# A two-layer decoder trunk on one core: the start and the scan re-ordered, and modulation columns summed from transposed weights

## The chip, the core and the metric

The kernel runs on one core of a Trainium2 chip. The metric is the time of one execution on the device in microseconds, the median of three runs. The core's engines are TensorE (PE in the profile; PEld is its loading of weights), VectorE (DVE), ScalarE (ACT), GpSimd (POOL) and SyncE (SP), which only issues transfers here.

## The reference, cut

All is f32: 512 tokens, 1024 channels. Both layers modulate their normed input by a shift and a scale and their output by a gate, all three computed from a conditioning vector c:

```python
mod = jax.nn.silu(c) @ w + b                      # (1024) @ (1024, 3072), per layer
shift, scale, gate = jnp.split(mod, 3, axis=-1)
...
h = rmsnorm(x, norm_g[l]) * (1.0 + scale) + shift
out = gated_deltanet_layer(...) if l == 0 else nsa_layer(...)
x = x + gate * out
```

Layer 0 is a gated DeltaNet: a projection to q, k, v (each with a causal convolution over 4 tokens and silu), to an output gate z and to decays; then a delta rule in chunks with a triangular solve per chunk, a scan over chunks that carries a 128 x 128 state per head, a norm, and an output projection. The stream after it gives shared keys and values; layer 1 is native sparse attention on these, and its own output projection. A last RMSNorm ends it.

## The kernel before, in words

**Dense products.** Channels lie on partitions, tokens in the free dimension. Each weight tile of 1024 x 128 is loaded (512 KB, tile `wraw`, a ring of three) and split into a high and a low part in fp32r (`split_w`), as is the activation. One output tile of 128 channels x 512 tokens is then 8 x 3 matmuls of 512 columns: high weight on high activation, low on high, high on low (`dense_steps`, lines 190, 192, 194). The high part is made on ScalarE; the low one by a subtraction on VectorE and GpSimd, or, with `adds`, by a negated copy on ScalarE and a transfer of GpSimd's queue that adds the weight to it (line 164).

**Order.** The order on TensorE is written by hand. Latency-bound work (the decay tables, the inverse, the doubling, the scan) is written with calls of `fill(n)` in it, each of which issues the next n matmuls from the list `todo` of dense tiles. `Ahead` wraps a tile, loads its weights one or two tiles early and splits them. ScalarE's order is by hand too in the middle of the program; those of VectorE, GpSimd and SyncE come from a scheduler with priorities (`tc.high_priority`).

**Stages of layer 0.** First the gain (1 + scale) x norm of layer 0 is summed on TensorE from four chunks of modulation weights (`chunk`, `vec_mat`, `ada`: matmuls at line 334 in four row groups, a copy on VectorE at 336, transposes at 340, a reduction at 341). Behind each chunk, x times its gain is split (`xsh`, `xsl`) and two of eight row blocks of the first four key tiles are accumulated in four open banks (lines 450 to 452). Key tiles 4 to 7 follow (`key`), with the shift sums. The list `todo` then holds queries 0 to 2, output gates 0 to 3, query 3, values 0 to 3, queries 4 to 7, values 4 to 7, gates 4 to 7. Each query, key and value tile has convolution taps on VectorE (line 81). Between them run the decay tables and a 32 x 32 triangular inverse on VectorE, which is doubled on TensorE, `attn` for two groups of four heads, and `scan_step(n, G)` for four chunk pairs n and two groups G. `scan_norm` normalises the result. The output projection (`residual`, tiles x10 to x17) begins inside the scan: its first three tiles (`w0`, `p0`, `some`, lines 1054 to 1058) take the first halves of the rows as soon as they exist.

**Modulation pieces.** Everything but layer 0's gain and shift comes later, in 32 transfers of 512 KB (`ada_piece`, into the ring `wraw`). A piece is two row blocks of 512 columns, and VectorE adds each, times one silu(c) per partition, to a partial sum `ap` (line 81; the first of four pieces begins it on ScalarE). After four pieces, four TensorE transposes (line 387) and a reduction (389) give 512 columns. A piece is worked on when the next is called. `with_pieces` calls it at step 13 and at the end of a tile, for queries, values and gates 4 to 7 (24 pieces); `gate_b` in layer 1 calls the other eight.

## Time and profile before

| | us |
|---|---|
| runs | 794.82, 794.88, 793.02; median 794.82 |
| the profiled execution: its time | 796.41 |
| the profiled execution: its span | 794.6 |
| busy: TensorE, VectorE, ScalarE, GpSimd | 748.1, 567.9, 433.8, 277.3 |
| mean granted clock of TensorE | 0.981 |

The span runs from the first to the last instruction that the profiler saw. Busy times count overlapping instructions of one engine once. The granted clock is TensorE's share of full speed, 1.00 being 2.4 GHz. A wait is put down to the releaser that came last. "Line" is a line of the kernel before; a line such as 81 or 84 is a helper's, and the tile names tell which step it is.

### The profile page before, as it was taken

Reading aid. Unit: us, or ns where it says so; the run is one execution under the profiler, and the core shown is the slowest. Engines: PE = TensorE matmul, PEld = TensorE weight load, DVE = VectorE, ACT = ScalarE, POOL = GpSimd, SP = SyncE. Lnnn points to the kernel's source line nnn. Section 1 sums busy time; section 2 is a strip of 40 time slices with the busy share of each in tenths; the row PEclk is TensorE's granted clock in tenths of the full one; section 3 lists DMA queues with packets and bytes.
Section 4 is the critical chain, followed back from the end, with each engine's and each line's share of the span. In section 5 each row is a group of like instructions: output and inputs, shape, how many; then the busy total and the mean of one; then the engine's idle time right before and its main releaser. Section 6 shows DMA issues by size and latency. Waiting matters only on the chain.

```text
span 794.6 us, 13620 instructions
## 1 busy us (share of the span) xinstructions
PE 748.1 (94%) x4837; PEld 610.0 (77%) x4837; DVE 567.9 (71%) x1487; ACT 433.8 (55%) x955; POOL 277.3 (35%) x302
## 2 busy tenths in 40 slices
PE   3999999989999989799999999999999999999986
...
GB/s 298 392 217 206 60 147 153 180 91 122 201 177 189 229 218 54 196 110 193 207 124 169 106 81 93 93 67 94 93 67 67 67 80 133 107 54 146 28 40 107
DMA packets 41780, 108.38 MB, mean 136 GB/s; under 512 B 4522, under 2 KB 13034, under 8 KB 41712
## 3 DMA queue, kind: packets, MB, share of 16 engines
...
HBM read 103.26 MB, written 5.55 MB: 137 GB/s over the span
## 4 chain that ended last, share of the span: by engine, by line
PE 75%; DVE 11%; DMA 6%; ACT 3%; issue 2%; POOL 1%; SPq 0%; ACTq 0%; DVEq 0%; POOLq 0%
PE z L192 5%; PE z L190 5%; PE z L194 5%; DMA aw<-in_ada_w 4%; PE o L1300 4%; PE pt L1284 4%; PE pc L192 4%; PE pc L194 4%; PE pc L190 4%; PE x L194 2%; PE x L192 2%; PE x L190 2%; PE q L192 2%; PE q L194 2%; PE q L190 2%
## 5 line engine op out<-in xcount | busy, mean ns | idle before, releaser
L84 POOL TENSOR_TENSOR wlo<-wraw,whi 128x512 fp32r<-128x512 f32 (+2 forms) x60 | 95.2, 1589 | 120.7 <-ACT whi L87 71.3
L87 ACT ACTIVATE arX<-arX,nm 128x256 f32<-128x256 f32 (+3 forms) x128 | 71.2, 556 | 104.3 <-DVE nm L1241 103.7
L87 ACT ACTIVATE whi<-wraw 128x1024 fp32r<-128x1024 f32 (+2 forms) x85 | 88.3, 1040 | 37.5 <-DMA wraw<-in_wS 9.9
L78 POOL TENSOR_SCALAR arX<-arX,f 128x256 f32<-128x256 f32 (+3 forms) x128 | 68.0, 544 | 99.4 <-DVE f L84 53.7
L194 PE MATMUL z<-h1l,whi 128*128 128x512 f32 x192 | 76.8, 400 | 0.0
L190 PE MATMUL z<-h1h,whi 128*128 128x512 f32 x192 | 76.6, 399 | 0.0
L192 PE MATMUL z<-h1h,wlo 128*128 128x512 f32 x192 | 75.9, 396 | 0.0
L84 DVE TENSOR_TENSOR wlo<-wraw,whi 128x512 fp32r<-128x512 f32 (+3 forms) x57 | 58.5, 1029 | 8.2 <-ACT whi L87 8.0
L81 DVE SCALAR_TENSOR_TENSOR ap<-aw,csil,ap 128x512 f32<-128x512 f32 x56 | 43.7, 781 | 26.7 <-DMA aw<-in_ada_w 25.0
L164 POOL DMA_DIRECT2D wlo<-in_wA x22 | 19.2, 872 | 123.9 <-ACT wlo L87 87.9
L190 PE MATMUL pc<-xh,whi 128*128 128x512 f32 x128 | 52.4, 409 | 3.5 <-DVE vT L81 3.5
L192 PE MATMUL pc<-xh,wlo 128*128 128x512 f32 x128 | 53.1, 415 | 0.0
L194 PE MATMUL pc<-xl,whi 128*128 128x512 f32 x128 | 52.1, 407 | 0.0
L1284 PE MATMUL pt<-ident,arX 128*128 128x128 f32 x320 | 45.3, 272 | 0.0
L1284 PEld LDWEIGHTS pt<-ident,arX 128*128 128x128 f32 x320 | 38.8, 140 | 8.3
L192 PEld LDWEIGHTS z<-h1h,wlo 128*128 128x128 f32 x192 | 36.1, 188 | 6.1
L190 PEld LDWEIGHTS z<-h1h,whi 128*128 128x128 f32 x192 | 36.2, 188 | 5.6
L194 PEld LDWEIGHTS z<-h1l,whi 128*128 128x128 f32 x192 | 36.1, 188 | 5.5
L1241 DVE CUSTOM_DVE_ANT_0 arX<-sw,arY 128x256 f32<-128x256 f32 (+2 forms) x48 | 26.7, 556 | 11.6 <-POOL arX L78 6.2
L1270 DVE TENSOR_SCALAR f<-sm 128x3 f32<-128x3 f32 x64 | 15.8, 246 | 24.5 <-ACT arX L87 24.2
L1300 PE MATMUL o<-pta,vb 128*64 128x128 f32 x336 | 32.1, 275 | 0.0
L190 PEld LDWEIGHTS pc<-xh,whi 128*128 128x128 f32 x128 | 24.7, 193 | 8.7 <-issue 3.9
...
## 6 DMA issues: line engine op xcount, KB each, us to landing
wraw<-in_wB SPq DMA_DIRECT2D x33, 512.0 KB, 3.3
aw<-in_ada_w SPq DMA_DIRECT2D x32, 512.0 KB, 4.9
wraw<-in_wA SPq DMA_DIRECT2D x28, 512.0 KB, 3.6
wlo<-in_wA POOLq DMA_DIRECT2D x22, 512.0 KB, 7.1
wraw<-in_wO SPq DMA_DIRECT2D x8, 512.0 KB, 4.0
...
wraw<-in_wP SPq DMA_DIRECT2D x8, 512.0 KB, 3.3
wraw<-in_wKV SPq DMA_DIRECT2D x6, 512.0 KB, 3.3
```

The costliest lines, as they stand in the source:

```text
L78: eng.tensor_scalar(out=o, in0=i, scalar1=s1, scalar2=s2, op0=op0, op1=op1)
L81: nc.vector.scalar_tensor_tensor(out=o, in0=i, scalar=s, in1=j, op0=op0, op1=op1)
L84: eng.tensor_tensor(out=o, in0=a, in1=b, op=op)
L87: nc.scalar.activation(o, i, fn, **kw)
L164: nc.gpsimd.dma_start(lo, src, accum_op=ALU.add)
L190: nc.tensor.matmul(ps, wh[:, k], xh[:, k], start=(k == 0), stop=False)
L192: nc.tensor.matmul(ps, wl[:, k], xh[:, k], start=False, stop=False)
L194: nc.tensor.matmul(ps, wh[:, k], xl[:, k], start=False, stop=(k == KT - 1))
L1241: nc.vector.tensor_tensor_reduce(out=o, in0=ps, in1=bias, op0=ALU.add, op1=ALU.min, scale=1.0, scalar=init, accum_out=acc)
L1270: nc.vector.tensor_scalar_max(f[:, qb], sm[:, qb], 1e-30)
L1284: nc.tensor.transpose(self.ps[:, i], x[:, kb * P:(kb + 1) * P], ident)
L1300: nc.tensor.matmul(po[64 * e:64 * e + 64, qb * P:(qb + 1) * P], vv, pts[2 * pr + e, br, kb, qb], start=(kb == 0), stop=(kb == qb), tile_po ...
```

## The change

- **Start.** The gain comes in eight slices of 128 columns, each with its rows of x and of the key weights, one ahead of the product that uses it: `gain_sums`, `gain` and `key_weights` for row block k + 1 are issued around the matmuls of block k. Sums are copied out of PSUM on ScalarE. The key weights that the shift's projection needs later stay where they are, so their second loading (`again`) is gone. The shift sums stand inside key tiles 4 and 5. Some small tables move from GpSimd's queue to SyncE's; the vector of ones is one column.
- **Pieces.** The host stores the modulation weights transposed too (`ada_r`): a piece holds whole rows of 1024 for 128 columns, and one `tensor_tensor_reduce` on VectorE, against silu(c) spread to all partitions (`csr`), gives 128 finished columns. Partial sums, transposes and reductions are gone. There are still 32 pieces of 512 KB: eight with queries 4 to 7, one with each of values and gates 4 to 7, eight with the output projection's tiles 3 to 7 (two, two, two, one, one), and eight in `gate_b`.
- **Order.** Output gate 3 stands behind value 0 instead of before query 3. The values' transposes of head 1 move behind `attn(0)`.
- **Scan.** The scan's own VectorE operations get a high priority (`first`). The multiplications of `scan_norm` for the first group are on ScalarE. The first three output weights are loaded and split early, as three entries `outs`, with the adding transfer.

```diff
+    csr = cp.tile([P, KT * P], F32, name="csr")
+    nc.gpsimd.dma_start(csd.rearrange("k p -> p k"), csil)
+    nc.gpsimd.dma_start(csr, csd.rearrange("k p -> (k p)").partition_broadcast(P))
...
+    def ada_piece():
...
+        q, j = i // 4, i % 4
...
+        w = wp.tile([P, KT * P], F32, name=f"aw{i}", tag="wraw", bufs=3)
+        nc.sync.dma_start(w, A["ada_r"][l, 4 * q + j])
...
         def add():
...
-            if k == 0:
-                part[0] = tp.tile([P, T], F32, name=f"ap{i}", tag="ap", bufs=1) if space is None else space[:, 2048:][:, :T]
-            for e in range(2):
-                c = csil[:, k + e:k + e + 1]
-                if k + e == 0:
-                    act(part[0], w[:, e], scale=c)
-                else:
-                    stt(part[0], w[:, e], c, part[0], ALU.mult, ALU.add)
-            if k == 6:
-                due.append(partial(finish, part[0]))
-
-        def finish(part):
-            ps = bank(f"as{i}")
-            for j in range(4):
-                nc.tensor.transpose(ps[:, j], part[:, j * P:(j + 1) * P], ident)
-            m = mod[:, l, 4 * q:4 * q + 4]
-            nc.vector.tensor_reduce(out=m, in_=ps, axis=AX.X, op=ALU.add)
-            tt(nc.vector, m, m, adab[:, l, 4 * q:4 * q + 4], ALU.add)
-
-        while loaded:
-            loaded.pop(0)()
+            c = 4 * q + j
+            nc.vector.tensor_tensor_reduce(out=w, in0=w, in1=csr, op0=ALU.mult, op1=ALU.add, scale=1.0,
+                                           scalar=adab[:, l, c:c + 1], accum_out=mod[:, l, c:c + 1])
...
+    chunks = [spaces[k // 4][:, k % 4 * 1024:][:, :1024].rearrange("p (k f) -> p k f", k=KT) for k in range(KT)]
+    for k in range(KT):
+        nc.sync.dma_start(chunks[k], A["ada_s"][k])
+        if k == 0:
+            nc.sync.dma_start(ident, A["ident"])
+        nc.sync.dma_start(xT[:, k], xsrc[:, k])
+        nc.sync.dma_start(wk[0][:, k], A["wS"][k])
...
+    def gain_sums(k):
+
         with tc.high_priority(offset=200):
-            ada(0, 8 + 2 * i, chunks[i])
-            stt(gs[:, 0, kk], mod[:, 0, 8 + 2 * i:10 + 2 * i], 1.0, normg[:, 0, kk], ALU.add, ALU.mult)
-        for k in (2 * i, 2 * i + 1):
+            ps = pm.tile([P, P], F32, name=f"gain{k}", tag="m")
+            for i in range(KT):
+                g = i % 4
+                nc.tensor.matmul(ps[32 * g:32 * g + 32], square_of(csil[:, i:i + 1], 32), chunks[k][:, i], start=(i < 4), stop=(i >= 4), tile_position=(0, 32 * g))
+            sums0[k] = tmp(f"gainp{k}", (P, P))
+            act(sums0[k], ps)
+
+    def gain(k):
+
+        with tc.high_priority(offset=200):
+            ps = pm.tile([P, P], F32, name=f"gainc{k}", tag="m")
+            nc.tensor.transpose(ps, sums0[k], ident)
             g = gs[:, 0, k:k + 1]
+            nc.vector.tensor_reduce(out=g, in_=V(ps, 0, [[32, 4]]), axis=AX.X, op=ALU.add)
+            nc.vector.tensor_scalar(out=g, in0=g, scalar1=adab1[:, k:k + 1], scalar2=normg[:, 0, k:k + 1], op0=ALU.add, op1=ALU.mult)
             act(xh[:, k], xT[:, k], scale=g)
             stt(xl[:, k], xT[:, k], g, xh[:, k].bitcast(F32), ALU.mult, ALU.subtract)
-        for k in ((), (0, 1, 2, 3), (4, 5, 6, 7), ())[i]:
-            square(k)
-        if i == 2:
+
+    parts0 = {}
+
+    def key_weights(k):
+        if k % 2 == 0:
+            parts0[k] = [wp.tile([P, 2, T], F32R, name=n, bufs=3) for n in ("whi", "wlo")]
+        hi, lo = (t[:, k % 2] for t in parts0[k - k % 2])
+        act(hi, wk[0][:, k])
+        tt(nc.gpsimd if k % 2 else nc.vector, lo, wk[0][:, k], hi.bitcast(F32), ALU.subtract)
+        return hi, lo
+
+    gain_sums(0)
+    gain(0)
+    for k in range(KT):
+        hi, lo = key_weights(k)
+        if k + 1 < KT:
+            gain_sums(k + 1)
+        for i, (w, x) in enumerate(((hi, xh), (lo, xh), (hi, xl))):
+            for c, ps in enumerate(open_ps):
+                nc.tensor.matmul(ps, w[:, c * P:(c + 1) * P], x[:, k], start=(i == 0 and k == 0), stop=(i == 2 and k == KT - 1))
+            if i == 0 and k + 1 < KT:
+                gain(k + 1)
+        for j in ((), (), (0,), (1, 2), (3, 4), (5, 6, 7), (), ())[k]:
+            square(j)
+        if k == 5:
             ps0 = pm.tile([P, T], F32, name="rs0ps", tag="m")
-            nc.tensor.matmul(ps0, ones, acc, start=True, stop=True)
+            nc.tensor.matmul(ps0, square_of(ones), acc, start=True, stop=True)
             rs0 = rows_rstd(ps0, "rs0")
-        wh, wl = split_w(raws[i], 2, split=(i == 0))
-        for c, ps in enumerate(open_ps):
-            for e in range(2):
-                k = 2 * i + e
-                nc.tensor.matmul(ps, wh[:, 2 * c + e], xh[:, k], start=(k == 0), stop=False)
-                nc.tensor.matmul(ps, wl[:, 2 * c + e], xh[:, k], start=False, stop=False)
-                nc.tensor.matmul(ps, wh[:, 2 * c + e], xl[:, k], start=False, stop=(k == KT - 1))
-
-
-    raws = [load_w(A["wA"][4])]
-    shw = []
-    for i, tag in enumerate("XV"):
-        shw.append(chunk(A["ada_w"][0, i], T, arenas[tag]))
-        raws.append(load_w(A["wA"][5 + i]))
-    raws.append(load_w(A["wA"][7]))
+
+    shw = [arena(t, f"sh{t}").rearrange("p (k f) -> p k f", k=KT) for t in ("xh", "xl")]
+    raws = []
+    for h in range(4):
+        raws.append(wk[1][:, :, h * P:(h + 1) * P])
+        nc.sync.dma_start(raws[h], A["wA"][4 + h])
+        for k in range(0, KT, 2) if h < 2 else ():
+            nc.sync.dma_start(shw[h][:, k:k + 2], A["ada_w"][0, h][:, k:k + 2])
+    nc.sync.dma_start(rows, A["rows"].partition_broadcast(P))
+    for t, n in ((cst, "cst"), (wab, "wab"), (rbt, "rb"), (pos, "pos")):
+        nc.sync.dma_start(t, A[n])
+
...
+    def key(h, *between):
+
+        between = list(between)
+        if h < 4:
+            ps = open_ps[h]
+        else:
+            for i, ps in enumerate(dense_steps(None, xsh, xsl, f"pc{h}", 2, raw=raws[h - 4], ahead=False)):
+                if i % 12 == 11 and between:
+                    between.pop(0)()
         kn[h] = tmp(f"kn{h}")
         tt(nc.vector, kn[h], ps, rs0, ALU.mult)
 
...
+    key(4, partial(shift_sums, 0), partial(shift, 0))
+    taps(0, kT[:, 0], kn[0])
+    taps(1, kT[:, 1], kn[1])
+    key(5, partial(shift_sums, 1), partial(shift, 1))
+    xh, xl = by8(arena("xh", "xh", F32R)), by8(arena("xl", "xl", F32R))
+    shifted(0)
+    taps(2, kT[:, 2], kn[2])
+    taps(3, kT[:, 3], kn[3])
+    shifted(1)
+    key(6)
...
-    def with_pieces(steps):
+    def with_pieces(steps, n=1):
 
         for i, s in enumerate(steps):
             if i == 13:
                 ada_piece()
             yield s
-        ada_piece()
+        if n > 1:
+            ada_piece()
 
...
-    for f, heads in ((query, (0, 1, 2)), (gate_proj, (0, 1, 2, 3)), (query, (3,)), (value, (0, 1, 2, 3)), (query, (4, 5, 6, 7)), (value, (4, 5, 6, 7)),
+    for f, heads in ((query, (0, 1, 2)), (gate_proj, (0, 1, 2)), (query, (3,)), (value, (0,)), (gate_proj, (3,)), (value, (1, 2, 3)), (query, (4, 5, 6, 7)), (value, (4, 5, 6, 7)),
                      (gate_proj, (4, 5, 6, 7))):
         todo += [Ahead(f(h), early=f is not query or h > 1) for h in heads]
+    w0 = {}
+
+    def ahead_x1(j):
+
+        raw = load_w(A["wO"][j])
+        yield None
+        w0[j] = split_w(raw, src=A["wO"][j])
+        yield None
+        p0.append((pd if j < 2 else pm).tile([P, T], F32, name=f"x1{j}", tag="d" if j < 2 else "s"))
+        yield from some(j, range(4), every, False)
+
+    outs = [Ahead(ahead_x1(j), early=True) for j in range(3)]
     fill(7)
 
+    nA = cp.tile([P, 8], F32, name="nA")
+    act(nA, rows[:, 0:8], AF.Exp)
...
-    fill(100)
-    for h in range(2):
-        fill((50, 24)[h])
-        value_rows(h)
+    fill(126)
+    value_rows(0)
+    fill(48)
...
+    first = partial(tc.high_priority, offset=600)
...
-            tt(nc.vector, kd, psk, bc(erest[:, sl4, n], P), ALU.mult)
+            with first():
+                tt(nc.vector, kd, psk, bc(erest[:, sl4, n], P), ALU.mult)
...
-            tt(nc.vector, vN[:, sl4, n], vN[:, sl4, n], bc(rs[:, :, n - n0], P), ALU.mult)
+            if G:
+                tt(nc.vector, vN[:, sl4, n], vN[:, sl4, n], bc(rs[:, :, n - n0], P), ALU.mult)
+            else:
+                for i in range(4):
+                    act(vN[:, i, n], vN[:, i, n], scale=rs[:, i, n - n0:n - n0 + 1])
...
-        for h in (2, 3):
+        for h in (1, 2, 3):
...
-        w0 = [split_w(load_w(A["wO"][j])) for j in range(3)]
-        p0 = [(pd if j < 2 else pm).tile([P, T], F32, name=f"x1{j}", tag="d" if j < 2 else "s") for j in range(3)]
+        p0 = []
...
-        todo += [some(j, range(4), every, False) for j in range(2)]
+        todo += outs[:2]
...
-            todo.append(some(2, range(4), every, False))
+            todo.append(outs[2])
...
-        tiles = [Ahead(t) for t in tiles]
+        tiles = [Ahead(with_pieces(t, 2 if i < 3 else 1)) for i, t in enumerate(tiles)]
```

The first place is the start of TensorE's program; `ada_8` and `gain` are sums of layer 0's gain, `pc` the open banks of the key tiles. Before:

```order
L334 MATMUL ada_8_137<-arX,scb 32x256 x8
L340 MATMUL ada_8c<-ident,ada_8p 128x128 x2
L450 MATMUL pc_132<-xsh,whi 128x512
L451 MATMUL pc_132<-xsh,wlo 128x512
L450 MATMUL pc_133<-xsh,whi 128x512
L450 MATMUL pc_134<-xsh,whi 128x512
L450 MATMUL pc_135<-xsh,whi 128x512
L451 MATMUL pc_135<-xsh,wlo 128x512
L451 MATMUL pc_133<-xsh,wlo 128x512
L451 MATMUL pc_134<-xsh,wlo 128x512
L334 MATMUL ada_10_189<-arX,scb 32x256 x4
L452 MATMUL pc_132<-xsl,whi 128x512
```

Now:

```order
L389 MATMUL gain_141<-asxh,csil 32x128 x8
L397 MATMUL gainc_152<-ident,gainp_150 128x128
L389 MATMUL gain_162<-asxh,csil 32x128 x8
L422 MATMUL pc_132<-xsh,whi 128x512
L422 MATMUL pc_133<-xsh,whi 128x512
L422 MATMUL pc_134<-xsh,whi 128x512
L422 MATMUL pc_135<-xsh,whi 128x512
L397 MATMUL gainc_177<-ident,gainp_171 128x128
L422 MATMUL pc_132<-xsh,wlo 128x512
L422 MATMUL pc_133<-xsh,wlo 128x512
L422 MATMUL pc_134<-xsh,wlo 128x512
L422 MATMUL pc_135<-xsh,wlo 128x512
```

The first key product moved behind the second slice's sums, and a slice now runs through the four banks before the next slice's begins.

The second place is VectorE at `attn(1)`: `qk` products are multiplied into `arN` there, and `pha` is a small norm table. Before:

```order
L81 SCALAR_TENSOR_TENSOR ap_2522<-aw_2495,csil,ap_2522 128x512
L81 SCALAR_TENSOR_TENSOR ap_2522<-aw_2520,csil,ap_2522 128x512
L544 COPY pha<-sstq 128x16 x2
L81 SCALAR_TENSOR_TENSOR ap_2522<-aw_2520,csil,ap_2522 128x512
L84 TENSOR_TENSOR arN_803<-qk_2573,arN_803 128x512
L78 TENSOR_SCALAR nx_2557<-pha 128x32
L81 SCALAR_TENSOR_TENSOR ap_2522<-aw_2601,csil,ap_2522 128x512
L84 TENSOR_TENSOR arN_803<-qk_2579,arN_803 128x512
L303 TENSOR_SCALAR pha<-nx_2557 128x32
L84 TENSOR_TENSOR arN_803<-qk_2585,arN_803 128x512
L81 SCALAR_TENSOR_TENSOR ap_2522<-aw_2601,csil,ap_2522 128x512
L84 TENSOR_TENSOR arN_803<-qk_2591,arN_803 128x512
```

Now (an ISA row is a piece, with `mod 128x1` as its sum's read-out):

```order
L542 COPY pha<-sstq 128x16 x2
L78 TENSOR_SCALAR nx_2545<-pha 128x32
L303 TENSOR_SCALAR pha<-nx_2545 128x32
L78 TENSOR_SCALAR pha<-pha 128x32
L84 TENSOR_TENSOR arN_854<-qk_2561,arN_854 128x512
L81 SCALAR_TENSOR_TENSOR nw_2546<-pha 128x32
L340 ISA aw_2711,mod<-aw_2711,csr,colp 128x1024
L340 ISA mod 128x1
L84 TENSOR_TENSOR arN_854<-qk_2567,arN_854 128x512
L84 TENSOR_TENSOR nw_2546<-nw_2546,nx_2545 128x32
L84 TENSOR_TENSOR arN_854<-qk_2573,arN_854 128x512
L84 TENSOR_TENSOR arN_854<-qk_2579,arN_854 128x512
```

Five additions for pieces became one row sum between the same products.

The third place is SyncE's queue from the last layer 0 tiles into the output projection (`aw` a piece, `wraw` a weight). Before:

```order
L370 DMA aw_2495<-in_ada_w 128x1024
L370 DMA aw_2520<-in_ada_w 128x1024
L370 DMA aw_2601<-in_ada_w 128x1024
L370 DMA aw_2648<-in_ada_w 128x1024
L370 DMA aw_2709<-in_ada_w 128x1024
L370 DMA aw_2761<-in_ada_w 128x1024
L370 DMA aw_2791<-in_ada_w 128x1024
L370 DMA aw_2820<-in_ada_w 128x1024
L156 DMA wraw<-in_wO 128x1024 x6
L1076 DMA arK<-in_xT 128x2x512 x2
L156 DMA wraw<-in_wO 128x1024 x2
```

Now:

```order
L336 DMA aw_2494<-in_ada_r 128x1024
L156 DMA wraw<-in_wO 128x1024
L336 DMA aw_2589<-in_ada_r 128x1024
L156 DMA wraw<-in_wO 128x1024
L336 DMA aw_2711<-in_ada_r 128x1024
L156 DMA wraw<-in_wO 128x1024
L336 DMA aw_2787<-in_ada_r 128x1024
L156 DMA wraw<-in_wO 128x1024 x3
L1094 DMA arK<-in_xT 128x2x512 x2
L336 DMA aw_3163<-in_ada_r 128x1024
L336 DMA aw_3185<-in_ada_r 128x1024
L156 DMA wraw<-in_wO 128x1024
```

Three output weights moved in between the pieces, and pieces now follow among the later output weights.

## Rows read from the trace of the kernel before

**Rows 1.** The page: busy time by engine, and the chain that ended last.

```profile
PE 748.1 (94%) x4837; PEld 610.0 (77%) x4837; DVE 567.9 (71%) x1487; ACT 433.8 (55%) x955; POOL 277.3 (35%) x302
...
PE 75%; DVE 11%; DMA 6%; ACT 3%; issue 2%; POOL 1%; SPq 0%; ACTq 0%; DVEq 0%; POOLq 0%
```

**Rows 2.** Windows: PE, PEld, DVE, ACT, POOL busy (instructions), PE clock, DMA share, GB/s.

```profile
20.00:40.00 20.00, 18.47 (x106) 12.91 (x107) 11.86 (x23) 13.75 (x20) 5.42 (x4) 1.00 1.01 392
40.00:60.00 20.00, 18.56 (x99) 12.54 (x98) 18.75 (x23) 6.99 (x10) 15.94 (x12) 1.00 0.69 211
160.00:180.00 20.00, 16.48 (x207) 13.92 (x207) 9.48 (x11) 10.25 (x14) 4.59 (x5) 0.66 0.42 94
280.00:300.00 20.00, 16.25 (x100) 14.23 (x99) 12.87 (x39) 5.35 (x17) 0.86 (x1) 0.91 0.75 200
320.00:340.00 20.00, 14.39 (x85) 12.50 (x84) 16.93 (x35) 7.64 (x21) 8.97 (x8) 0.83 0.63 211
```

**Rows 3.** Waits by engine: us in total, times, longest us.

```profile
PE x L1056 <- DVE wlo L84: 5.5, 1, 5.5
...
PE pc L190 <- DVE vT L81: 3.5, 1, 3.5
...
DVE ap L81 <- DMA aw<-in_ada_w: 25.0, 14, 5.4
...
POOL S L84 <- PE qs L915: 21.9, 2, 16.6
```

**Rows 4.** TensorE's timeline, start: start us, us, line, operands, count, [idle before].

```profile
8.70 1.08 PE L334 MATMUL ada<-arX,scb 128*32 128x256 f32 x8 [8.70 <-DMA arX<-in_ada_s]
...
9.93 1.08 PE L334 MATMUL ada<-arX,scb 128*32 128x256 f32 x8 [0.15 <-DMA arX<-in_ada_s]
...
15.12 0.80 PE L450 MATMUL pc<-xsh,whi 128*128 128x512 f32 x1 [2.87 <-ACT xsh L87]
...
16.14 1.48 PE L450 MATMUL pc<-xsh,whi 128*128 128x512 f32 x3
...
33.50 1.08 PE L450 MATMUL pc<-xsh,whi 128*128 128x512 f32 x4
...
34.41 1.02 PE L444 MATMUL rs0ps<-rs0acc,ones 128*128 128x512 f32 x2
...
41.36 1.92 PE L334 MATMUL ada<-arX,scb 128*32 128x512 f32 x16
...
50.52 0.39 PE L190 MATMUL pc<-xsh,whi 128*128 128x512 f32 x1
```

**Rows 5.** Timelines of VectorE and ScalarE, start.

```profile
12.68 0.16 DVE L81 SCALAR_TENSOR_TENSOR gs<-mod,colp 128x2 f32<-128x2 f32 x1
...
14.37 1.32 ACT L87 ACTIVATE xsh<-arA,gs 128x512 fp32r<-128x512 f32 x2
```

**Rows 6.** Groups by form: busy us, mean ns of one, idle before.

```profile
L84 DVE TENSOR_TENSOR wlo<-wraw,whi 128x512 fp32r<-128x512 f32 x47 | 47.5, 1013 | 2.3 <-ACT whi L87 2.0
...
L81 DVE SCALAR_TENSOR_TENSOR ap<-aw,csil,ap 128x512 f32<-128x512 f32 x56 | 43.7, 781 | 26.7 <-DMA aw<-in_ada_w 25.0 <-ACT ap L87 1.3
...
L81 DVE SCALAR_TENSOR_TENSOR sl<-arK,colp,sh 128x512 fp32r<-128x512 f32 x8 | 11.8, 1481 | 3.8 <-ACT sh L87 3.8
...
L1241 DVE CUSTOM_DVE_ANT_0 arX<-sw,arY 128x512 f32<-128x512 f32 x16 | 11.0, 690 | 8.1 <-POOL arX L78 6.2 <-PE sw L1233 0.9 <-PE sd L1233 0.4
...
L81 DVE SCALAR_TENSOR_TENSOR arK<-x,mod,arK 128x512 f32<-128x512 f32 x8 | 6.0, 747 | 6.1 <-PE x L194 4.5 <-PE x L1058 1.6
...
L387 PE MATMUL as<-ident,ap 128*128 128x128 f32 x32 | 4.8, 274 | 0.0
```

**Rows 7.** VectorE's timeline in the inverse.

```profile
145.04 0.75 DVE L81 SCALAR_TENSOR_TENSOR arA<-pc,colp,arA 128x509 f32<-128x509 f32 x1 [0.72 <-ACT arA L87]
```

**Rows 8.** DMA issues: queue, count, KB each, median us to landing.

```profile
aw<-in_ada_w SPq DMA_DIRECT2D x32, 512.0 KB, 4.9
...
x1d<-arK ACTq DMA_DIRECT2D x8, 256.0 KB, 2.4
```

149 lines of the change are left out of this document (53 added, 96 removed).

## The prediction

> **What bounds the kernel now.** I read four views, each for one question. First the page's busy times: TensorE is busy for 748.1 of 794.6 us [rows 1], so what it issues in the dense products can't shrink much, and a gain has to come from its idle time, from half-rate stretches, or from instructions that it need not issue. The page's chain confirms it: three quarters of the path that ended last is TensorE, 11% VectorE, and 6% DMA, of which the modulation pieces are most [rows 1]. So I looked next where TensorE is not full, by windows of 20 us [rows 2], and then for the cause of each hole in the waits by engine [rows 3]. Four places stand out:
> - The start. The first key product runs at 15.12 us, and the fifth key tile, the first that is an ordinary dense tile, begins at 50.52 us [rows 4].
> - 160 to 180 us: one wait of 3.5 us for a convolution tap on VectorE [rows 3], and a mean granted clock of 0.66 behind it [rows 2], between the two levels of 1.2 and 2.4 GHz, so that some two thirds of the stretch ran at the lower.
> - 280 to 300 us, the second half of the scan: 16.25 of 20 us busy, clock 0.91 [rows 2].
> - 320 to 340 us: 14.39 of 20 us busy, clock 0.83 [rows 2]; the low half of an output weight comes 5.5 us late from VectorE [rows 3].
>
> The profiled execution took 796.41 us, 1.59 above the median of 794.82. The sum is made against 796.41 and the 1.59 is taken off at its end.
>
> **The start.** Before, the gain comes in four chunks of 256 columns, the key weights in four parts. After, everything comes in eight slices of 128 columns, each 1 MB (512 KB of modulation weights, 256 KB of x, 256 KB of key weights). The DMA engines moved 392 GB/s from 20 to 40 us [rows 2], so a slice takes 2.6 us of them and the last lands at about 8.7 + 7 x 2.6 = 27 us, before TensorE can use it. The first row sums can begin when the first chunk did, at 8.70, and take at most the 1.08 of the wider ones [rows 4]: 9.78. From the end of the second half of the sums before (9.93 + 1.08 = 11.01 [rows 4]) to the finished gain (12.68 + 0.16 = 12.84 [rows 5]) lie 1.83 us; a scaled slice of x is another 0.66, half of 1.32 [rows 5]. So the first key product starts at 9.78 + 1.83 + 0.66 = 12.3 us. The first products before ran three in 1.48 us [rows 4]; twelve of these are 5.9, to 18.2. Later four take 0.91 (33.50 to 34.41 [rows 4]), so a slice is 12 x 0.23 = 2.76 us, with half of 1.08 for the next sums and 0.15 for one transpose (4.8 us over 32 [rows 6]): 3.45. Seven of them end at 42.4; the sum of squares adds 1.02 [rows 4], to 43.4. The fifth key tile thus starts 7.1 us earlier than at 50.52. But the first shift sums, 1.92 us before it [rows 4], now stand inside it: **5.2 us** gained. Bounds: 8 with sums half as long and no half-rate products, and 0, because VectorE was busy for 18.75 of 20 us from 40 to 60 [rows 2] and could simply become what the key tiles wait for. I take the sum, since the copies of the sums leave VectorE for ScalarE, which was busy for only 6.99 us there [rows 2].
>
> The re-load of 4 MB of key weights disappears behind other work: nothing. The shared silu row adds a small write and a 512 KB spread read on GpSimd's queue, but the first piece comes with the fifth query tile, twelve dense tiles of 5.5 us after the keys: nothing.
>
> **The doubling stall.** TensorE has the same steps to fill up to the 3.5 us wait [rows 3]. On VectorE the inverse, with convolution taps woven in, is the same chain but for one wait of 0.72 us on ScalarE [rows 7]. I take **0.7**. Bounds: 0, and 3.5 + 16.48 x 0.34 = 9.1 if the whole stall and the slow stretch behind it go [rows 2, 3].
>
> **Scan.** Before, 24 of the 32 pieces fall on the projections beside the scan, two per tile; after, 16, with one per value and gate tile. VectorE waited 25.0 us in 14 places for these transfers [rows 3]. The steps of the scan's chain are also put first on VectorE, and a normalisation of sixteen squares goes to ScalarE, busy for 5.35 of 20 us [rows 2]. From 280 to 300 us TensorE lost 3.75 us idle and 16.25 x 0.09 = 1.5 in clock: **5.2** gained. Bounds 2 and 7: with fewer pieces something else in the chain may come late, and the two stretches beside it also have some idle time.
>
> **The output weights at 320 us.** Three tiles are now loaded and split before, ScalarE making the high halves and an adding DMA of GpSimd's queue the low ones. Lost in this window: 5.6 idle and 14.39 x 0.17 = 2.4 in clock, 8.0 [rows 2]. The next late things are short ones, so I leave 1 us for them: **7.0**. Bounds 0 and 8. What is queued on GpSimd matters: the loads that add stand in one queue with multiplications of the state, which waited 21.9 us in two places for TensorE [rows 3].
>
> **Pieces.** Each was two fused multiply-adds of 0.781 us [rows 6], with four transposes and a reduction per four pieces. Now each is one multiplication with a running sum over 1024 elements. The softmax's instructions with a maximum do 512 elements in 0.690 us [rows 6], so I take 1.38; bounds 0.69 (one of that size) and 1.56 (both old ones). Where they stay beside the dense tiles, VectorE has room: nothing. The 32 transposes leave TensorE; their group is 4.8 us busy [rows 6], of which a third are tails under the next product: **3.2** gained, bounds 0 and 4.8.
>
> Eight of them now fall on five output tiles. A tile is 24 x 0.23 = 5.5 us of TensorE, and has 1.01 + 0.75 + 1.48 = 3.24 us on VectorE (a low half, the residual, a shifted square input [rows 6]). Spare: 5 x 5.5 - 5 x 3.24 = 11.4 us. The waits before were 25.0 us over 32 pieces, 0.78 each [rows 3]. 8 x (0.78 + 1.38) = 17.3, so 5.9 us stick out: **minus 5.9**. Bounds: 0 if VectorE may run behind and catch up, and 8 x (25.0/14 + 1.38) - 11.4 = 13.9 if each waits as long as those that waited.
>
> **Sum.** 5.2 + 0.7 + 5.2 + 7.0 + 3.2 - 5.9 = 15.4; 796.41 - 15.4 = 781.0, and less 1.59 it is **779.4 us**.
>
> **Rivals.**
> - *The doubling stall goes.* The swapped gate and value tiles could let VectorE reach the last tap sooner, so that the clock never falls. For it: it needs only 3.5 us. Against: the same instructions stand before it. 8.4 us more than my 0.7: 771.0.
> - *VectorE binds the start.* For it: 18.75 of 20 us [rows 2]. Against: it loses copies. The 5.2 fall away: 784.6.
> - *The early halves are not early.* The adding loads sit behind a state multiplication on GpSimd's queue and the wait at 320 us stays as it is, so that the change doesn't do there what it says. 7.0 fall away: 786.4. Against: they are issued before the second half of the scan.
> - *Slower: pieces hold VectorE in the output projection.* With two pieces in 24 steps, 12 steps apart (2.8 us), and 4.9 us from issue to landing [rows 8], VectorE may stand at each piece with the residual of the tile, whose bank TensorE wants, queued behind. With 4.9 us of wait in each, 8 x (4.9 + 1.38) - 11.4 = 38.8 stand for my 5.9: 812.3. It decides from a wait w with 8 x (w + 1.38) - 11.4 = 21.3 (the other gains), w = 2.7 us. Against: before, where two pieces also stood in each tile, the longest was 5.4 but the mean 1.8 [rows 3].
> - *Slower: small transfers.* If the three transfers of a slice went one behind the other, each would be at least 4.9 + 2 x 2.4 = 9.7 us [rows 8], the last slice landing at 8.7 + 7 x 9.7 = 76.6, the fifth key tile starting at about 82 instead of 43.4: 39 us more, 818. Against: in the same stretch 512 KB transfers flowed at 392 GB/s [rows 2] though one alone takes 4.9 us [rows 8], so many are in flight. The Trainium skill, "DMA: Bandwidth & Descriptors", in its section on measured rates, advises batching DMAs to 1 MiB or more for three quarters of peak, and so speaks against pieces of 256 KB; by it the time would go towards this rival's 818, by the rate in the row it stays at 779.4, and I follow the row.
>
> **How the numbers follow.** Forecast 0.55, stall gone 0.14, start bound 0.13, halves not early 0.07, pieces hold VectorE 0.07, small transfers 0.04. Range: from 765, which is the stall rival's 771.0 less what the upper bounds of start, scan and transposes add (2.8 + 1.8 + 1.6 = 6.2), to 792, which is the halves' rival's 786.4 with the start's 5.2 gone too. It leaves out the two slow cases (0.11) and the tails of the others. 0.3% (2.4 us) is about what a measurement tells from no change. The two slow cases hold 0.11; a part of them with shorter waits, and the corner where several gains fail together, end within it: same 0.03, slower 0.09, faster 0.88.
>
> **What would show it.** First key product near 12.3 and fifth tile near 43.4 us; no TensorE wait for the low half near 320 us, and the 280 to 300 us stretch near full at clock 1.00; no transposes of partial sums; a piece near 1.4 us. Still a wait of about 3 us before the doubling. In the output projection, small TensorE waits for VectorE, 6 us in all. I am wrong if the waits for pieces there are above 2.7 us each, if the key tiles wait for VectorE, or if the wait at 320 us is still there.

## The result, and the profile after

The changed kernel takes 798.38 us (median of 9 runs, 796.77 to 802.68), the kernel before 793.02 in 9 runs of the same comparison (791.09 to 794.88). The ratio is 1.0073, with a 95% interval of 1.0055 to 1.0090: **slower by 0.7%**, where 779.4 was forecast. Executions of one kernel differ by up to 10 us here, so a difference of 2 us or less is read from the intervals, not from two profiles.

The page of the changed kernel: busy times, and the group of the modulation pieces.

```profile
PE 746.1 (94%) x4869; PEld 607.5 (76%) x4869; DVE 557.0 (70%) x1467; ACT 437.8 (55%) x978; POOL 278.1 (35%) x299
...
L340 DVE CUSTOM_DVE_ANT_0 aw<-aw,csr,colp 128x1024 f32<-128x1024 f32 x32 | 43.3, 1352 | 37.8 <-DMA aw<-in_ada_r 31.2
```

TensorE is busy for 2.0 us less than in [rows 1] in a span of the same 794.6 us: what was taken off it went into waits. A piece is one instruction of 1.35 us in the mean, as predicted (1.38); its transfers still hold VectorE for 31.2 us in all.

The windows of 20 us (columns as in [rows 2]) show where:

```profile
60.00:80.00 20.00, 14.54 (x64) 10.87 (x57) 17.08 (x27) 14.36 (x22) 5.11 (x4) 0.83 0.09 27
160.00:180.00 20.00, 16.44 (x169) 14.00 (x168) 15.52 (x16) 11.88 (x14) 6.35 (x6) 0.80 0.50 113
280.00:300.00 20.00, 19.29 (x112) 15.13 (x110) 9.37 (x29) 8.43 (x20) 1.72 (x2) 1.00 0.60 159
320.00:340.00 20.00, 19.55 (x135) 17.06 (x135) 15.16 (x37) 10.32 (x32) 5.60 (x6) 1.00 0.56 174
360.00:380.00 20.00, 17.37 (x76) 13.80 (x74) 16.96 (x22) 6.09 (x9) 8.56 (x6) 1.00 0.80 276
```

and the first of these windows in the kernel before:

```profile
60.00:80.00 20.00, 20.00 (x97) 14.82 (x96) 19.09 (x27) 15.81 (x24) 6.17 (x4) 1.00 0.66 210
```

From 280 to 300 and from 320 to 340 us TensorE is nearly full at clock 1.00, against 16.25 and 14.39 us and lower clocks before [rows 2]: the scan did gain. From 60 to 80 us, which was full before, it is busy for 14.54 us at 0.83, and from 360 to 380, in the output projection, for 17.37. The stretch at 160 to 180 us is as before but for its clock.

The waits of TensorE, and four rows of its timeline at the start:

```profile
PE gain L389 <- DMA asxh<-in_ada_s: 10.8, 3, 5.5
PE shiftc L485 <- ACT shiftp L87: 5.5, 1, 5.5
PE pc L190 <- DVE vT L81: 3.6, 1, 3.6
...
PE kv L192 <- POOL wlo L84: 1.9, 1, 1.9
...
PE kv L190 <- ACT whi L87: 1.7, 1, 1.7
...
PE x L190 <- DVE arK L81: 0.9, 1, 0.9
```

```profile
5.55 0.87 PE L389 MATMUL gain<-asxh,csil 128*32 128x128 f32 x12 [5.55 <-DMA asxh<-in_ada_s]
...
17.90 0.64 PE L389 MATMUL gain<-asxh,csil 128*32 128x128 f32 x16 [4.17 <-DMA asxh<-in_ada_s]
...
48.34 0.50 PE L190 MATMUL pc<-xsh,whi 128*128 128x512 f32 x1
...
69.67 1.12 PE L485 MATMUL shiftc<-ident,shiftp 128*128 128x128 f32 x4 [5.46 <-ACT shiftp L87]
```

The first sums begin at 5.55 us, earlier than the forecast 8.70, and then the third slice's sums stand at 17.90 for a transfer; the fifth key tile begins at 48.34 us (43.4 forecast, 50.52 before [rows 4]); and the second shift sums are waited for 5.5 us. The wait ahead of the doubling is still there, 3.6 us. The last three waits belong to the output projection (`x`) and the key-value tiles behind it (`kv`).

Four groups of matmuls mark the stages (duration in ns, then first and last start in us): the decay sums `psab`, the queries' sums of squares `ssq`, the last state update `su`, and the key-value tiles `kv`.

```profile
L642 PE MATMUL psab<-arA,pha x16: 592/592/617, 84.4 to 85.8; 128*32 128x512 f32 x16
...
L529 PE MATMUL ssq<-sqarA,pha x16: 592/604/617, 243.7 to 280.9; 128*32 128x512 f32 x16
...
L952 PE MATMUL su<-vp,kd x48: 270/275/377, 239.5 to 328.0; 128*128 128x128 f32 x48
...
L190 PE MATMUL kv<-sh,whi x48: 387/389/628, 379.8 to 423.3; 128*128 128x512 f32 x48
```

The same marks, from the same view, of six kernels (us; "before" in two executions, the second is e10; the kernels e6 to e14 are explained below):

| | before | before, again | after | e6 | e7 | e9 | e14 |
|---|---|---|---|---|---|---|---|
| decay sums begin | 77.0 | 76.1 | 84.4 | 78.0 | 77.6 | 72.6 | 72.5 |
| last `ssq` | 272.2 | 270.4 | 280.9 | 276.0 | 273.4 | 275.2 | 269.1 |
| last `su` | 332.9 | 327.5 | 328.0 | 323.0 | 320.3 | 321.3 | 315.4 |
| first `kv` | 381.6 | 376.3 | 379.8 | 375.0 | 372.8 | 374.3 | 367.2 |
| span | 794.6 | 788.9 | 794.6 | 788.9 | 785.7 | 788.5 | 782.4 |

Read by differences: the change loses 7.4 to 8.3 us before the decay sums and 1.3 to 2.2 from there to the last `ssq`; gains 10 to 14 in the second half of the scan (47.1 us from `ssq` to `su`, against 60.7 and 57.1); loses 3.0 from there to the first `kv` and 4.2 in the key-value tiles (50.5 us from the first `kv` to the first query of layer 1, against 46.3 in both); and gains 2.0 to 2.5 in layer 1.

What fills the hole at the start: windows of 2 us of the changed kernel,

```profile
10.00:12.00 2.00, 2.00 (x7) 1.46 (x7) 0.30 (x2) 0.00 (x1) 0.00 (x0) 1.00 1.31 85
12.00:14.00 2.00, 1.73 (x8) 1.08 (x6) 0.35 (x2) 0.00 (x0) 0.00 (x0) 1.00 0.95 88
14.00:16.00 2.00, 0.00 (x0) 0.00 (x0) 0.00 (x0) 0.00 (x0) 0.00 (x0) 1.00 0.96 103
16.00:18.00 2.00, 0.10 (x4) 0.13 (x8) 0.00 (x0) 1.13 (x2) 0.41 (x1) 1.00 0.85 127
```

and two of them in the kernel before:

```profile
10.00:12.00 2.00, 1.45 (x10) 0.42 (x10) 0.42 (x1) 0.00 (x0) 0.00 (x0) 1.00 1.02 382
...
16.00:18.00 2.00, 2.00 (x6) 1.52 (x6) 1.39 (x3) 0.00 (x0) 0.00 (x0) 1.00 1.04 407
```

GpSimd's timeline in the same stretch,

```profile
3.96 1.11 POOL L322 DMA_DIRECT2D csd<-csil  x1 [3.51 <-DVE csil L84]
17.59 0.60 POOL L323 DMA_DIRECT2D csr<-csd  x1 [12.52 <-DMA csd<-csil]
18.29 1.29 POOL L84 TENSOR_TENSOR wlo<-arX,whi 128x512 fp32r<-128x512 f32 x1
```

and the transfer in the list of DMA issues (queue, count, size, us from issue to landing):

```profile
csd<-csil POOLq DMA_DIRECT2D x1, 4.0 KB, 13.3
```

From 10 to 18 us the DMA engines are busy for 85 to 131% of their time by the records and move 85 to 127 GB/s, where the kernel before moved 382 to 410 in the same windows. The one thing in flight that the kernel before didn't have is a write of 4 KB, the silu of c, in single elements: 13.3 us from issue to landing. GpSimd stood 12.5 us for it, with the low half of the second slice's weights queued behind (18.29); and SyncE's queue, which waited 7.2 us for one slice's key weights to land, issued nothing from 9.60 to 16.86 us.

And VectorE from 50 to 66 us:

```profile
50.86 12.45 DVE L81 SCALAR_TENSOR_TENSOR arK<-kn,colp,arK 128x509 f32<-128x509 f32 x11
63.23 0.68 DVE L84 TENSOR_TENSOR kn<-pc,rs 128x512 f32<-128x512 f32 x1
63.83 0.16 DVE L487 TENSOR_REDUCE mod<-shiftc 128x4 f32<-128x16 f32 x1
...
65.44 0.16 DVE L84 TENSOR_TENSOR mod<-mod,colp 128x4 f32<-128x4 f32 x1
```

Eleven convolution taps (12.45 us) and the fifth tile's normalisation stand ahead of the reduction of the first shift sums, which TensorE had ready at 56.6. ScalarE, whose copy of the second shift sums is queued behind work that needs the first shift, is late in turn, and TensorE with it.

### The profile page after: what moved, and what is told of

It is laid out like the page before. It is cut to its first block, busy times and chain, and to the rows that moved or that the text cites. A ratio compares the mean times of both kernels' runs of the same rounds, so it can differ in the third digit from the quotient of the medians.

```text
span 794.6 us, 13653 instructions
## 1 busy us (share of the span) xinstructions
PE 746.1 (94%) x4869; PEld 607.5 (76%) x4869; DVE 557.0 (70%) x1467; ACT 437.8 (55%) x978; POOL 278.1 (35%) x299
## 3 DMA queue, kind: packets, MB, share of 16 engines
HBM read 101.16 MB, written 5.55 MB: 134 GB/s over the span
## 4 chain that ended last, share of the span: by engine, by line
PE 55%; DVE 5%; DMA 3%; ACT 3%; issue 3%; POOL 1%; ACTq 0%; DVEq 0%; POOLq 0%; SPq 0%
PE z L190 5%; PE z L192 5%; PE z L194 5%; PE o L1318 5%; PE pt L1302 4%; DMA aw<-in_ada_r 3%; PE q L194 2%; PE q L192 2%; PE q L190 2%; PE kv L192 2%; PE kv L194 1%; PE kv L190 1%; PE sw L1250 1%; PE sw L1251 1%; PE oc L1333 1%
## 5 line engine op out<-in xcount | busy, mean ns | idle before, releaser
L84 POOL TENSOR_TENSOR wlo<-wraw,whi 128x512 fp32r<-128x512 f32 (+1 forms) x49 | 80.4, 1643 | 89.2 <-ACT whi L87 60.4
L87 ACT ACTIVATE whi<-wraw 128x1024 fp32r<-128x1024 f32 (+1 forms) x77 | 80.6, 1047 | 16.9 <-DMA wraw<-in_wKV 5.8
L192 PE MATMUL z<-h1h,wlo 128*128 128x512 f32 x192 | 76.1, 396 | 0.0
L340 DVE CUSTOM_DVE_ANT_0 aw<-aw,csr,colp 128x1024 f32<-128x1024 f32 x32 | 43.3, 1352 | 37.8 <-DMA aw<-in_ada_r 31.2
L84 DVE TENSOR_TENSOR wlo<-wraw,whi 128x512 fp32r<-128x512 f32 (+1 forms) x45 | 48.6, 1080 | 1.9 <-ACT whi L87 1.7
L1302 PEld LDWEIGHTS pt<-ident,arX 128*128 128x128 f32 x320 | 38.8, 140 | 8.3
L1288 DVE TENSOR_SCALAR f<-sm 128x3 f32<-128x3 f32 x64 | 14.1, 221 | 24.3 <-ACT arX L87 23.9
```

The lines of the kernel that those rows point to most:

```text
L84: eng.tensor_tensor(out=o, in0=a, in1=b, op=op)
L87: nc.scalar.activation(o, i, fn, **kw)
L192: nc.tensor.matmul(ps, wl[:, k], xh[:, k], start=False, stop=False)
L340: nc.vector.tensor_tensor_reduce(out=w, in0=w, in1=csr, op0=ALU.mult, op1=ALU.add, scale=1.0, scalar=adab[:, l, c:c + 1], accum_out=mod[:, ...
L1288: nc.vector.tensor_scalar_max(f[:, qb], sm[:, qb], 1e-30)
L1302: nc.tensor.transpose(self.ps[:, i], x[:, kb * P:(kb + 1) * P], ident)
```

## The experiments

**1. The start, first round.** e1 moves the two transfers of silu(c) behind the key tiles in the text; e2 sets VectorE's order by hand, six taps and then the reduction; e3 is both; e4 has the start of the kernel before with all the rest.

```diff
# e1
-    nc.gpsimd.dma_start(csd.rearrange("k p -> p k"), csil)
...
     dump("h", xT)
+    nc.gpsimd.dma_start(csd.rearrange("k p -> p k"), csil)
# e2
-    key(4, partial(shift_sums, 0), partial(shift, 0))
+    def between_taps():
+        with order("DVE"):
+            for h in range(2):
+                taps(h, kT[:, h], kn[h])
+            shift(0)
+            for h in (2, 3):
+                taps(h, kT[:, h], kn[h])
+
+    key(4, partial(shift_sums, 0), between_taps)
```

> The changed kernel, with the two transfers that spread silu(c) to all partitions issued behind the key tiles instead of first of all. Theory A: the write of 1024 single elements holds the DMA engines from 10 to 18 us, and with it the third slice and, on GpSimd's queue, the low half of the second slice. Then the stretch of 85 to 130 GB/s is gone, the fifth key tile starts at about 41 us instead of 48.3, and the time falls by 5 to 8 us, to about 791. Rival C: slices of 256 and 512 KB are slow in themselves, or VectorE binds the start: the fifth tile stays near 48 and the time near 798.

> The changed kernel, with the order on VectorE fixed so that the shift sums' reduction stands behind six taps instead of eleven. Theory B: the wait of TensorE for the second shift sums (5.5 us) comes from this queue, since ScalarE's copy of the sums stands behind work that needs the first shift. Then this wait is under 1 us, the clock stays up from 60 to 80 us, and the time falls by 5 to 8 us, to about 792. Rival: the taps that are moved back hold the next thing (the low half of a key weight), the wait reappears there, and the time falls by less than 2 us.

> Both edits. If the two losses are separate, as theories A and B say, the gains add up: 12 to 15 us, about 785. If one hides the other (the start is bound by one chain through VectorE), no more than the larger of the two single gains, about 791.

> The start as it was before (four chunks, re-loading of key weights, shift sums ahead of the fifth key tile), with all the rest of the change, and silu(c) spread behind the key tiles. If the start alone is what went wrong, the rest keeps what the traces show behind the start (7.5 us): about 785.5 against 793.0 of the kernel before. Rival: the rest gains only because the start is late and other engines catch up meanwhile; then about 792.

Measured: e1 799.74 (ratio to before 1.0100, 1.0077 to 1.0123), e2 794.77 (1.0028, 1.0010 to 1.0045), e3 794.46 (1.0027, 1.0008 to 1.0045), e4 794.32 (1.0024, 1.0007 to 1.0040). e2 is 3.6 us faster than the changed kernel, half of what was expected: the wait fell from 5.5 to 2.6 us, not away. e1 tested nothing: GpSimd's queue is in the scheduler's order, and the write was issued at 3.90 us again, as it was in e3 and, at 4.57, in e4. So e1 repeats the changed kernel and e3 repeats e2. e4 has the write with the old start, and its decay sums began at 83.3. So the loss before the decay sums needs no new slices.

**2. The row without memory.** e5 makes the spread row on TensorE, e6 adds e2's order, e7 is e4 with that row, e8 is e6 with the eight pieces of the output projection back at values and gates 4 to 7.

```diff
# e5 to e8, after the key tiles
-    nc.gpsimd.dma_start(csd.rearrange("k p -> p k"), csil)
-    nc.gpsimd.dma_start(csr, csd.rearrange("k p -> (k p)").partition_broadcast(P))
+    for i in range(2):
+        ps = pm.tile([P, T], F32, name=f"row{i}", tag="m")
+        for k in range(4):
+            nc.tensor.matmul(ps[:, k * P:(k + 1) * P], square_of(csil[:, 4 * i + k:4 * i + k + 1]), ident, start=True, stop=True)
+        act(csr[:, i * T:(i + 1) * T], ps)
# e8
-        tiles = [Ahead(with_pieces(t, 2 if i < 3 else 1)) for i, t in enumerate(tiles)]
+        tiles = [Ahead(t) for t in tiles]
```

> The earlier edit that put the two transfers of silu(c) later in the text did not move them: the scheduler of GpSimd's queue issued them at 3.9 us again, and the slow stretch stayed. Here the row is made without memory: eight 128-column products of silu(c) with the identity on TensorE and two copies on ScalarE, after the key tiles; about 2 us of new work. Theory A: the stretch of 85 to 130 GB/s between 10 and 18 us is gone, the fifth key tile starts near 41 us and the first decay sums near 78 instead of 84.4, and the time falls by 5 us from that of the changed kernel, to about 793. Rival C (small slices slow in themselves, or a start bound by VectorE): the stretch stays or the fifth tile does, and the time is 798 to 800.

> The row on TensorE, and the reduction of the shift behind six taps instead of eleven, as in the earlier run that gained 3.6 us by itself. If the two are separate: about 790. If the key tiles are bound by VectorE as soon as transfers are early, the second edit or the first gives nothing more and it is about 793.

> The start as before, with the rest of the change, and the row on TensorE: no write of single elements at all. Theory A says that the write also cost the run with the old start its 6 us (decay sums at 83.3 instead of 77.0). Then the decay sums begin near 78 and the time is about 789. If it stays at 794, the rest of the change gains nothing even from an undisturbed start.

> As the run with the row on TensorE and the shift first, but the eight pieces of the output projection are back with values and gates 4 to 7, two in each tile. Theory: those eight cost the output projection and the key-value tiles behind it 5 to 7 us (the predicted 5.9), and their return costs the scan up to 5.2: within 2 us of that run. Rival: the spreading was a loss, and this is faster by 4 us or more; or the scan loses all of its gain, and it is slower by 4 us or more.

Measured: e5 792.00 (1.0000, 0.9985 to 1.0015), e6 792.08 (0.9992, 0.9976 to 1.0009), e7 790.17 (0.9960, 0.9940 to 0.9979), e8 794.00 (1.0019, 0.9993 to 1.0045). In e5 the slow stretch is gone:

```profile
10.00:12.00 2.00, 2.00 (x6) 1.51 (x6) 0.33 (x2) 0.58 (x2) 1.27 (x1) 1.00 1.04 407
12.00:14.00 2.00, 2.00 (x7) 1.52 (x7) 1.17 (x4) 1.24 (x2) 0.00 (x0) 1.00 1.04 398
14.00:16.00 2.00, 2.00 (x23) 1.31 (x22) 0.58 (x1) 0.80 (x2) 0.00 (x0) 1.00 1.03 399
16.00:18.00 2.00, 2.00 (x11) 1.43 (x8) 0.77 (x3) 0.72 (x1) 1.28 (x1) 1.00 1.05 405
```

So the write and the read that waits for it cost 6.4 us (798.38 against 792.00; 5.8 by the ratios), and 4.2 with the old start (e4 against e7; 5.1 by the ratios). These are net of the new row, whose products stand on TensorE from 76.0 to 77.9 us in e5, just ahead of the decay sums. With the write gone, the new slices do what was forecast: the fifth key tile begins at 42.06 us in e5's timeline, but the shift sums are waited for again:

```profile
42.06 0.50 PE L190 MATMUL pc<-xsh,whi 128*128 128x512 f32 x1
...
61.46 0.90 PE L482 MATMUL shiftc<-ident,shiftp 128*128 128x128 f32 x3 [3.52 <-ACT shiftp L87]
```

8.5 us earlier at the fifth key tile than before (7.6 against e10), and no earlier at the decay sums (77.8): all of it is given back on the way, some 2 us of it to the row itself. e6 gained nothing on e5, as its second forecast had it (792.08 against 792.00); its wait for the second shift sums is still 2.6 us. Its trace shows what may hold it up. VectorE of e6, and below it GpSimd at the same time:

```profile
45.56 9.15 DVE L81 SCALAR_TENSOR_TENSOR arK<-kn,colp,arK 128x509 f32<-128x509 f32 x6
54.63 0.68 DVE L84 TENSOR_TENSOR kn<-pc,rs 128x512 f32<-128x512 f32 x1
55.24 0.16 DVE L484 TENSOR_REDUCE mod<-shiftc 128x4 f32<-128x16 f32 x1
...
57.03 5.06 DVE L81 SCALAR_TENSOR_TENSOR arK<-kn,colp,arK 128x509 f32<-128x509 f32 x6
```

```profile
39.32 12.55 POOL L84 TENSOR_TENSOR arA<-arA,rs 128x512 f32<-128x512 f32 x8 [3.39 <-DMA pha<-in_wab]
```

Six taps take 9.15 us, most of it while GpSimd multiplies x by the reciprocal norm (39.32 to 51.87), six later ones 5.06. If this is the chain, six taps ahead of the reduction are still too many, and so is the fifth tile's normalisation (54.63), which stands between them and the reduction; e9 tests it.

e8 against e6, by the marks: from the last `ssq` to the last `su` 53.6 us (280.9 to 334.5) against 47.0, and from there to the first `kv` 48.7 against 52.0, with the `kv` tiles taking 38.8 against 42.5. In these two profiles eight pieces fewer beside the scan are worth 6.6 us there, and cost 7.0 in the output projection and the tiles behind it. The same profiles also differ by 5.4 us between the decay sums and the last `ssq` (203.4 against 198.0), some of it because e8's profiled execution (795.39) was longer than its median and e6's (790.89) shorter. By the medians the move is worth 1.9 us, within the 2 that were expected, and the intervals overlap.

**3. The shift ahead, and what carried the scan.** e9 is e6 with the reduction behind three taps only and ahead of the normalisation. e10 is the kernel before, once more, for its profile. e11 is e7 with the first three output weights loaded and split late, as before; e12 is e7 without the scan's priority on VectorE and with all of `scan_norm` there.

```diff
# e9
+    dve = ExitStack()
+
+    def between_taps():
+        dve.enter_context(order("DVE"))
+        taps(0, kT[:, 0], kn[0])
+        shift(0)
+
+    key(4, partial(shift_sums, 0), between_taps)
+    for h in (1, 2, 3):
+        taps(h, kT[:, h], kn[h])
+    dve.close()
# e11
-        todo += outs[:2]
+        w0 = [split_w(load_w(A["wO"][j])) for j in range(3)]
+        todo += [some(j, range(4), every, False) for j in range(2)]
# e12
-    first = partial(tc.high_priority, offset=600)
+    first = ExitStack
-            if G:
+            if True:
```

> As the run with the row on TensorE and the shift behind six taps, but the shift's reduction now stands behind three taps only and ahead of the fifth key tile's normalisation. In that earlier run the fifth key tile began 7.5 us earlier than in the kernel before, yet the decay sums no earlier: TensorE waited 2.6 us for the second shift sums, with half-rate products behind the wait, because six taps took 9.2 us on VectorE while GpSimd multiplied x. If this chain is what gives the new start's gain back, the wait goes, the decay sums begin at 73 to 75 us instead of 78.0, and the time is 3 to 4 us lower, 788 to 789. Rival: VectorE as a whole binds this stretch, the taps come later for what follows, and the time stays at 792.

> The kernel before, unchanged, for a second profile. The first profiled execution took 796.4 us, 3.8 above the median of 35 runs (792.6). If executions differ by where TensorE waits and the clock falls behind a wait, a profile near the median shows less idle time or less half-rate time than [rows 2] at 280 to 300 or 320 to 340 us, together by some 3 us; if they differ elsewhere, these rows return within 0.5 us.

> As the run with the old start and the row on TensorE (790.2 us), but the first three output weights are loaded and split at the place where the kernel before did it. Predicted worth of this part: 7.0 us. If it is worth that, 797. Rival: in this kernel VectorE is free enough at 320 us that the low half is in time, or the early split costs elsewhere what it saves: 790 to 793.

> As the run with the old start and the row on TensorE (790.2 us), but without the high priority of the scan's own steps on VectorE and with the normalisation's multiplications all on VectorE. Predicted worth of the scan's part, with fewer pieces: 5.2 us. If the priority carries it, 795; if the smaller number of pieces beside the scan does, within 1.5 us of 790.2.

Measured: e9 **785.10** (0.9892, 0.9860 to 0.9925), e11 788.57 (0.9960, 0.9942 to 0.9977), e12 790.93 (0.9977, 0.9952 to 1.0002); e10's one execution 790.66. e9 confirms the chain. Its reduction starts at 50.34 us, five microseconds earlier than in e6, and TensorE is full from 40 to 80 us:

```profile
44.51 5.16 DVE L81 SCALAR_TENSOR_TENSOR arK<-kn,colp,arK 128x509 f32<-128x509 f32 x3
50.34 0.17 DVE L484 TENSOR_REDUCE mod<-shiftc 128x4 f32<-128x16 f32 x1 [0.67 <-PE shiftc L482]
```

```profile
40.00:60.00 20.00, 19.90 (x105) 13.28 (x104) 18.06 (x21) 12.35 (x18) 15.91 (x11) 1.00 0.46 183
60.00:80.00 20.00, 19.80 (x116) 13.46 (x118) 19.04 (x33) 12.40 (x21) 4.61 (x4) 1.00 0.40 105
```

The decay sums begin at 72.6 us, as expected, and e9 gains 7.0 us on e6, more than the 3 to 4 expected. It beats both kernels. Its one profile has a span of 788.5, the longest of its six executions, so its later stages are not read here; e14, the same start with late output weights, keeps the gain to the first `kv` (367.2 us, against 372.8 in e7).

e11 says that the early output weights are worth nothing in this kernel: with them loaded late TensorE doesn't wait for the low half, and the window that held the 5.5 us wait [rows 2, 3] is nearly full,

```profile
320.00:340.00 20.00, 18.69 (x132) 16.82 (x130) 14.61 (x36) 6.72 (x24) 6.38 (x8) 1.00 0.45 154
```

and e11 is no slower than e7 (equal ratios, within some 2 us). e12 is 0.8 us slower than e7 by the medians and 1.3 by the ratios: the priority and ScalarE's share of the norm aren't worth the 5.2, though up to some 4 lie within the intervals. Of the 10.0 to 13.6 us of the scan's gain e8 puts 6.6 down to the place of eight pieces. What carries the rest isn't shown. The wait for the low half is gone in e11 (late split, 16 pieces beside the scan) and in e8 (early split, 24 pieces); no run has the late split beside 24 of the new pieces. e10 is a warning about the sum's base: in this execution of the kernel before

```profile
280.00:300.00 20.00, 18.26 (x123) 15.87 (x121) 17.12 (x52) 4.52 (x15) 1.94 (x2) 1.00 0.56 161
300.00:320.00 20.00, 14.62 (x89) 11.74 (x89) 17.38 (x34) 8.31 (x21) 6.09 (x5) 0.97 0.27 81
320.00:340.00 20.00, 18.88 (x117) 17.34 (x118) 14.75 (x40) 6.53 (x23) 3.05 (x5) 0.86 0.69 224
```

the hole that stood at 280 to 300 us [rows 2] is smaller and the one behind it earlier, still with its 5.5 us wait for the low half, and the stage from `ssq` to `su` takes 57.1 us instead of 60.7: 3.6 less, as expected (some 3).

**4. What of the write it is.** e13 is the changed kernel with both transfers near the start, silu(c) transposed first, so that the write has eight lines of 128 elements. e14 is e9 with e11's edit.

```diff
# e13
+    nc.tensor.transpose(pst, csil, ident)
+    cs8 = tmp("cs8", (8, P))
+    act(cs8, pst)
-    nc.gpsimd.dma_start(csd.rearrange("k p -> p k"), csil)
+    nc.gpsimd.dma_start(csd, cs8)
```

> The changed kernel with both transfers kept at the start, but silu(c) is first transposed on TensorE, so that the write to memory is eight lines of 128 elements instead of 1024 single ones. If the single elements are what holds the other transfers, there is no stretch under 250 GB/s after 6 us and the time is that of the run with the row on TensorE (792.0) within 2 us. If any write to memory and reading back at this place does it (or GpSimd's queue, which waits for the write), the stretch or a late low half on GpSimd remains and the time is 796 or more.

> As the run with the shift ahead (785.1 us, the fastest so far), with the first three output weights loaded and split where the kernel before did it. If the early split is worth nothing here either, as in the run with the old start, within 2 us of 785.1; if its worth appears once the start is early, 790 or more.

Measured: e13 792.32 (0.9984, 0.9968 to 1.0000), e14 785.32 (0.9908, 0.9891 to 0.9924). Two windows of e13 and its write:

```profile
10.00:12.00 2.00, 2.00 (x15) 1.33 (x7) 0.75 (x1) 1.05 (x3) 0.60 (x1) 1.00 1.05 406
...
14.00:16.00 2.00, 2.00 (x23) 1.31 (x22) 1.34 (x2) 0.87 (x3) 0.62 (x1) 1.00 1.03 397
```

```profile
csd<-cs POOLq DMA_DIRECT2D x1, 4.0 KB, 5.5
```

Same bytes and same queue, and the other transfers run on at about 400 GB/s (397 to 412 from 8 to 20 us). So a write and a read back at the start need not hold the others; what is left is the single elements, with one reservation: e13's write waits for the transpose and is issued at 9.05 us instead of 3.96, still among the slices, and no run has the single elements at that later time. e14 is within its interval of e9's time (785.32 against 785.10): the early weights are worth nothing measurable there either.

## Why the prediction was wrong, by its steps

- **The step that failed** is one sentence of the start: "The shared silu row adds a small write and a 512 KB spread read on GpSimd's queue, but the first piece comes with the fifth query tile ...: nothing." It asked when the row is needed, and not what its write holds while it runs. It cost 6.4 us (e5), and e13, where the same bytes in lines cost nothing measurable, puts it down to the single elements, but for the later issue. With the next step it makes up most of the miss: of the 19.0 us between forecast and result 12.6 to 13.5 lie before the decay sums, where 5.2 were to be gained and 7.4 to 8.3 were lost. The Trainium skill, "DMA: Bandwidth & Descriptors", in its rules for kernel authors, says that a transfer with a last dimension that isn't contiguous becomes one descriptor per element. The trace doesn't count descriptors; it agrees as far as it goes, 13.3 us for 4 KB in single elements against 5.5 in lines. The harm to the transfers beside it is read from the traces alone.
- **The start, 5.2 us forecast.** The sum was near up to the fifth key tile (43.4 forecast, 42.06 in e5), partly by luck: the first key product began 2.7 us early (9.64 in e5, 12.3 forecast) and the slices took 1.3 us longer than summed. It was wrong behind the tile: it took the gain through to the end by subtracting the moved shift sums (1.92), and did not follow the chain shift sums, VectorE, ScalarE that now begins later than the key tile instead of earlier. The rival "VectorE binds the start" had the place, with 13%, but not the reason: VectorE's order bound it, not its load. With the order mended TensorE is full from 40 to 80 us with VectorE about as busy as before (18.06 and 19.04 of 20 us), and the forecast 5.2 appear (e9, 785.1, against e7, 790.2; decay sums at 72.6 against 77.6).
- **The doubling stall**: 0.7 forecast, none found (3.6 us of wait after, 3.5 before); within its bounds.
- **Scan and output weights, 5.2 + 7.0.** Together 12.2 forecast, 10.0 to 13.6 measured in the changed kernel. The size was right and the attribution wrong: the 7.0 were given to the early split alone, but without it e7 and e9 are no slower (e11, e14); the priority is worth little (e12), and the place of the pieces 6.6 (e8). That the late split is in time because there are fewer pieces on VectorE and in the DMA queues is likely, but argued.
- **Pieces in the output projection, 5.9 lost**: 7.2 in the changed kernel and 7.0 by e8 against e6, so the size was near, but by luck: the mechanism was another. VectorE waited 2.1 us in all for the transfers of the eight pieces there, at most 0.75 for one (0.78 each forecast, 2.7 for the slower rival), and TensorE waited only 0.9 us for VectorE where some 6 were forecast. The loss is in the key-value tiles: their first weight is issued at 373.96 us, behind the last pieces in SyncE's queue, and at 360.45 in the kernel before; TensorE waits 1.7 and 1.9 us for its two halves, and its granted clock is 0.50 to 0.69 from 380 to 388 us. None of this was in the sum. A piece at 1.35 us was right.
- **Transposes, 3.2**: from the first query of layer 1 to the end the changed kernel takes 357.0 us (430.3 to 787.3), the kernel before 359.0 to 359.5, with eight of the 32; for the others no run separates them from the pieces, and no row shows the third that was taken off as tails.
- **Small transfers**: the 256 and 512 KB slices flow at 398 to 407 GB/s in e5, so that rival is out. The prediction's sentence from the Trainium skill, with its 1 MiB, pointed towards 818; these rates show that it did not bear on slices of which many are in flight.
- **The base.** 796.41 was one of the longest executions of the kernel before, and part of the scan's hole belonged to that execution (e10). With the write and the order mended e9 and e14 are still 5.7 to 5.9 us above the 779.4; e14's profile still has 196.6 us from the decay sums to the last `ssq` and 50.6 in the key-value tiles.

Not settled: between the decay sums and the last `ssq` the changed kernel and e6 take 196.5 and 198.0 us, the kernel before 194.3 and 195.2. TensorE waits there for VectorE's products of the attention (2.5 us in e6); no run took this apart.
